# First norm's shift row summed on TensorE, four tiles scaled by ScalarE, and another order of the gate and up products

## The chip, the cores and the metric

The kernel runs on one core of one Trainium2 chip. The metric is the device time of one execution in microseconds (us). Before the change it is 2370.89 us, the median of three runs (2370.7 to 2372.88).

## The reference

The reference is a trunk of two layers on x of 1024 rows (tokens) by 1024 columns in float32, with a conditioning vector c of 1024. Cut to what matters here:

```python
c_act = silu(c)
for l in range(2):
    mod = (c_act @ ada_w[l] + ada_b[l])            # 6 * 1024 values
    sh1, sc1, g1, sh2, sc2, g2 = split(mod, 6)
    h = rms_norm(x, norm1_w[l]) * (1.0 + sc1) + sh1
    proj = h @ w_in[l]                             # 1824 columns
    ... three head groups: windowed attention, latent attention, spatial gating
    x = x + g1 * (y @ w_out[l])
    h = rms_norm(x, norm2_w[l]) * (1.0 + sc2) + sh2
    gate, up = split(h @ w_gate_up[l], 2)          # 2 * 2816 columns
    x = x + g2 * ((silu(gate) * up) @ w_down[l])
return rms_norm(x, final_norm_w)
```

The change touches two places: the first norm of layer 0, with `sc1` and `sh1` and the first projection's start, and the products of gate and up in both layers.

## The kernel before

**Arithmetic.** Large products are made of float32 values that are split in a high part, rounded to the fast float32 form, and a low part, the rest. `mm3` then issues three matmuls for one: high by high (L134), low by high (L135), high by low (L136). A part of 128x512 is one matmul. Operands that are split need two instructions: a cast to the high part (ACT, `TH`, `gus`) and a subtraction for the low part (`sub`, L139, `TL`).

**First norm of layer 0.** The 1024 rows are eight tiles of 128. Each tile is loaded (`load_x0`, L229), normalised on ACT (`normalise`, L235 and L237) and transposed on PE (`transposed`, L294, eight 128x128 pieces in two PSUM banks `hT`), and ACT copies the two banks to SBUF (`xT`, L295). The modulation comes from `ada_w`: for the shift (j = 0) and the scale (j = 1), and for each half of 512 columns, four loads of 256 rows by 512 columns, 512 KB each (`ada0w`, L265). Each brings two blocks of 128 rows, and DVE multiplies each with a value of `c_act` per partition and adds it up (`ada_mac`, L254 and L256, 32 in all). At the end of a half `reduce0` transposes the sums on PE (L281), DVE adds up over what were partitions (L283) and adds the bias (L284, and L286 for the scale). The result, `mod0`, holds a scale and a shift for each column of x, one value per partition after the transpose. `modulate` then scales a half of a tile: four pieces by DVE (L613), the high part by ACT (L616), the low part by POOL (L139).

**The first projection.** `w_in`'s columns 512 to 1023 come first (`wr`, loaded by `load_w1` at L570, split to `wh` and `wl`). Each tile needs 24 matmuls on its bank `avq`: twelve for the first half of the modulation, twelve for the second. `avq_end` evacuates a tile by three instructions of ACT (L649, L651, L655) and a DMA (`cq`, L652). Tiles 0 to 3 (`NE` = 4) can begin with the first half of the modulation alone; the others, and their loads of x, come behind both halves.

**Order.** Each engine works its instructions in the program's order. For the start of layer 0 that order is written out by hand in the string `PRS`: each letter stands for one step of a sequence (X a load of x, N a normalisation, t a tile's transposes, a and b the sums of the two halves, r a reduction, m a modulation, l a load of `w_in`, s a split, h, v, G, B the projections). `need("r", 2)` lets a sequence run another one up to a step. A buffer is held back until some work is done by a copy of one element (`after`, L304): DVE writes it to the buffer that a DMA will fill, so SP, which issues all DMAs here one after the other, waits for DVE at that point.

**Gate and up.** The gate and up product is a scheme with seven products in place of eight per pair of column blocks (11 pairs a layer). `left` yields the seven operands, of which some are sums and differences made on POOL; ACT casts and DVE subtracts to split them. A product is 24 matmuls, 12 to a bank `gate` and 12 to a bank `up`. Three pairs of banks are in use: `yy`, `xx` and `vv`. `yy` accumulates products 0, 3, 4 and 5, `vv` products 2 and 6, and `xx` product 1. Between two products of `yy` ACT copies its state out (`u`, L1523 after product 3, L1528 after product 4; `p1` after product 0).

Of the kernel before, what the change touches and what calls it, by code (L numbers as in the profile page):

```python
# [49 lines left out]
PRS = "XtaaaaNtNsatNlrbthmhmbhasmbNbGmbbNllblCmtmmsbmNhtGvaamrtvvmvmNmmGvvNmBBGsvBCBv"  # L50
SP0 = (1, 1, 0, 0)
MA = (0, 0, 0, 0)
# [14 lines left out]
EY = (1, 0, 1, 1, 0, 0, 0, 1)  # L67
AHEAD = (4, 2, 6, 10, 7, 9, 9)
# [10 lines left out]
def tile_trunk(ctx, tc, x, c, positions, ada_w, ada_b, norm1_w, w_in, a_sinks, b_q_norm_w, b_w_uq,  # L79
# [50 lines left out]
    def f32(t):  # L130
        return t.bitcast(F32)
# [117 lines left out]
    acc0 = {j: G([P, D], F32, "acc0") for j in (1, 0)}  # L249
# [20 lines left out]
    def macs0(raws, hf):  # L270
        for j, kp, raw in raws:
            a = acc0[j][:, hf * 512:(hf + 1) * 512]
            for k in range(2):
                ada_mac(a, raw[:, k, :], 2 * kp + k)
            yield

    def reduce0(hf):
        for j in (1, 0):
            pt = PA("ada0")
            for i in range(4):  # L280
                PE.transpose(chunk(pt, i), chunk(acc0[j], 4 * hf + i), ident)  # L281
            d = slice(8 * j + 4 * hf, 8 * j + 4 * hf + 4)
            DVE.reduce_sum(out=mod0[:, d], in_=pt.rearrange("p (a b) -> p a b", a=4), axis=AX.X)  # L283
# [5 lines left out]
    def transposed(xn):  # L289
        r = G([P, KD, P], F32, "xT")  # L290
        for kh in range(2):
# [3 lines left out]
            ACT.copy(out=r[:, 4 * kh:4 * kh + 4], in_=pv)  # L295
# [257 lines left out]
    def layer(l, x_tiles):  # L553
# [49 lines left out]
        def modulate(t, kh):  # L603
# [4 lines left out]
            for kk in range(4 * kh, 4 * kh + 4):  # L608
                if kk - 4 * kh < MA[2 * (t >= NE) + kh]:
                    ACT.activation(out=xa[:, kk, :], in_=xa[:, kk, :], func=AF.Identity, scale=mod0[:, 8 + kk:9 + kk],  # L610
                                   bias=mod0[:, kk:kk + 1])
                else:
# [4 lines left out]
            sub(POOL, lo[:, ks_], xa[:, ks_], f32(h[:, ks_]))  # L617
# [40 lines left out]
        if l == 0:  # L658
# [17 lines left out]
            def t_seq():  # L676
                for t in range(NT):
                    need("N", t + 1)
                    xT0[t] = transposed(xns.pop(t))
                    yield  # L680
# [725 lines left out]
        def left(a11, a12, a21, a22, tmp, tt):  # L1406

            yield a11
            yield a12
            tt(a11, a11, a21, ALU.subtract)  # L1410
            yield a11
            tt(tmp, a22, a11, ALU.subtract)
            yield tmp
            tt(a21, a21, a22, ALU.add)
            yield a21
            tt(a12, a12, tmp, ALU.subtract)
            yield a12
            yield a22
# [42 lines left out]
        def gu_prep(raws):  # L1461
            gens = []
            for r0, r1 in raws:
                tmp = AD("s2").rearrange("p (k c) -> p k c", k=4)
                gens.append(left(r0[:, :, 0, :], r1[:, :, 0, :], r0[:, :, 1, :], r1[:, :, 1, :], tmp, tt_on(POOL)))
# [16 lines left out]
        def gu_pair(j, ops, ahead):  # L1482

            p1 = G([P, 2, 512], F32, "p1")
            u4, u2 = [None, None], [None, None]
# [4 lines left out]
            def products(i, name, ps, first):  # L1490
                ahead(i)
                w = ops(i)
# [12 lines left out]

            yy = banks()
            yield from products(0, "b11", yy, True)
            for m in range(2):
                ACT.copy(out=p1[:, m, :], in_=yy[m])
            yield  # L1510
            xx = banks()
            yield from products(1, "b21", xx, True)
            for m in range(2):
                DVE.tensor_tensor(out=p1[:, m, :], in0=p1[:, m, :], in1=xx[m], op=ALU.add)
            finish(p1[:, 0, :], p1[:, 1, :], 0, 0)
            yield
            vv = banks()
            yield from products(2, "t3", vv, True)
            yield
            yield from products(3, "t2", yy, False)  # L1520
            for m in range(2):
                u2[m] = SM([P, 512], F32, "u2")
                ACT.copy(out=u2[m], in_=yy[m])  # L1523
            yield
# [258 lines left out]
```

## Time and profile before

| what | before |
|---|---|
| median of three runs | 2370.89 us |
| the profiled execution, its own time | 2370.5 us |
| its span | 2368.8 us |
| mean granted TensorE clock | 0.983 |
| first matmul of the first projection | at 33.19 us |
| second half of the modulation complete | at 51.4 us |
| last matmul of the first projection | from 95.32 us |
| gate and up, layer 0 and layer 1 (the windows read) | 531 to 987 and 1705 to 2143 us |

The profile is one execution, and its times are counted from the span's start. In a timeline a row gives the start, the time from there to the end, the engine, the line, the operation, what it writes and reads, how many instructions the row holds, and in brackets the idle time of the engine before it with what ended it. SPq rows are DMA issues. In a table of windows the columns are the window's ends, its length, the busy time and number of instructions of PE, PEld (weight loads), DVE, ACT and POOL, the granted TensorE clock as a share of the full one, the busy share of the DMA engines and GB/s. In a list of waits stand the us in total, the number of waits and the longest.

### The profile page before, as it was taken

How to read it: one execution, taken by the hardware profiler on the slowest of the kernel's cores; microseconds unless marked ns; L12 is line 12 of the kernel's file. 1: busy time of each engine (PE TensorE's matmuls, PEld its weight loads, DVE VectorE, ACT ScalarE, POOL GpSimd, SP SyncE). 2: the span in 40 equal slices, each digit the busy share in tenths (PEclk: the TensorE clock that was granted, in tenths of full speed). 3: DMA queues.
4: the chain of work that ended last, by engine and by line, in shares of the span. 5: the costliest groups of instructions: out<-in, count | busy, mean ns of one | idle time of the engine just before them, and what ended most of it. 6: DMA issues, size and time to landing. Idle time of an engine off the chain costs nothing. (4 is left out here: it accounts for less than half of the span.)

```text
span 2368.8 us, 31988 instructions
## 1 busy us (share of the span) xinstructions
PE 2258.4 (95%) x11191; PEld 1904.2 (80%) x11191; DVE 1775.4 (75%) x2793; ACT 1120.9 (47%) x2296; POOL 984.8 (42%) x997
## 2 busy tenths in 40 slices
PE   5999899999999999999999899999999999999998
PEld 4789798887888777878878788988878888887786
DVE  7787578848767777699974875687588767638978
ACT  4566377636344344323344654784564444432233
POOL 4766630322323324545554655212224334225643
PEclk9999999999999999999999999999999999999999
DMA  6503432212566565862240253222134544468433
GB/s 255 167 19 110 175 132 90 90 54 89 173 213 232 186 232 187 319 253 89 80 158 19 62 172 143 81 81 98 54 110 177 180 169 169 171 223 287 150 109 114
DMA packets 155397, 347.66 MB, mean 147 GB/s; under 512 B 12522, under 2 KB 71652, under 8 KB 155236
## 3 DMA queue, kind: packets, MB, share of 16 engines
q1 hardware_dynamic: 155236, 345.62, 42.2%
q8 instruction: 88, 1.44, 0.3%
q14 instruction: 73, 0.60, 0.1%
HBM read 250.65 MB, written 94.92 MB: 146 GB/s over the span
## 5 line engine op out<-in xcount | busy, mean ns | idle before, releaser
L139 DVE TENSOR_TENSOR gus<-gur,gus 128x512 fp32r<-128x512 f32 x264 | 248.3, 961 | 60.3 <-ACT gus L142 59.5
L142 ACT CAST gus<-gur 128x512 fp32r<-128x512 f32 x264 | 160.7, 624 | 209.7 <-PE gate L136 77.0
L134 PE MATMUL gate<-hTh,gus 128*128 128x512 f32 x616 | 243.9, 396 | 15.2 <-ACT hTh L142 8.1
L134 PE MATMUL down<-dnt,dns 128*128 128x512 f32 x616 | 241.8, 393 | 11.5 <-issue 6.0
L134 PE MATMUL up<-hTh,gus 128*128 128x512 f32 x616 | 241.1, 391 | 3.8 <-ACT u L1528 3.8
L135 PE MATMUL down<-dnt,dns 128*128 128x512 f32 x616 | 241.1, 391 | 1.3 <-DVE dnt L139 1.3
L135 PE MATMUL gate<-hTl,gus 128*128 128x512 f32 x616 | 241.7, 392 | 0.1
L136 PE MATMUL gate<-hTh,gus 128*128 128x512 f32 x616 | 241.2, 392 | 0.0
L136 PE MATMUL down<-dnt,dns 128*128 128x512 f32 x616 | 240.7, 391 | 0.0
L136 PE MATMUL up<-hTh,gus 128*128 128x512 f32 x616 | 240.4, 390 | 0.0
L135 PE MATMUL up<-hTl,gus 128*128 128x512 f32 x616 | 240.2, 390 | 0.0
L1435 POOL TENSOR_TENSOR gur<-gur 128x512 f32<-128x512 f32 x44 | 65.2, 1482 | 398.8 <-DVE gus L139 369.5
L142 ACT CAST dns<-act 128x512 fp32r<-128x512 f32 x132 | 81.8, 622 | 248.6 <-PE down L136 189.6
L1613 DVE TENSOR_TENSOR x<-x,down 128x512 f32<-128x512 f32 x224 | 148.0, 679 | 28.9 <-PE down L136 28.6
L134 PEld LDWEIGHTS gate<-hTh,gus 128*128 128x128 f32 x616 | 116.9, 190 | 43.4 <-ACT u L1523 10.0
L139 DVE TENSOR_TENSOR dns<-act,dns 128x512 fp32r<-128x512 f32 x132 | 136.3, 1047 | 15.5 <-ACT dns L142 15.3
L134 PEld LDWEIGHTS down<-dnt,dns 128*128 128x128 f32 x616 | 116.2, 189 | 38.5 <-issue 6.8
L134 PEld LDWEIGHTS up<-hTh,gus 128*128 128x128 f32 x616 | 116.1, 189 | 28.7 <-ACT u L1528 4.9
L135 PEld LDWEIGHTS down<-dnt,dns 128*128 128x128 f32 x616 | 116.5, 189 | 25.8 <-DVE dnt L139 1.7
L135 PEld LDWEIGHTS gate<-hTl,gus 128*128 128x128 f32 x616 | 116.8, 190 | 25.2 <-DVE hTl L139 1.5
L136 PEld LDWEIGHTS gate<-hTh,gus 128*128 128x128 f32 x616 | 116.7, 189 | 24.5
L136 PEld LDWEIGHTS down<-dnt,dns 128*128 128x128 f32 x616 | 116.5, 189 | 24.5
(415 smaller groups left out, 6132.8 us busy)
## 6 DMA issues: line engine op xcount, KB each, us to landing
gur<-in_w_gate_up_dram SPq DMA_DIRECT2D x88, 512.0 KB
ada<-in_ada_w_dram SPq DMA_DIRECT2D x80, 512.0 KB
wp<-wpe SPq DMA_DIRECT2D x77, 512.0 KB
dnt<-wp SPq DMA_DIRECT2D x77, 512.0 KB
dnr<-in_w_down_dram SPq DMA_DIRECT2D x44, 512.0 KB
act<-act SPq DMA_DIRECT2D x44, 512.0 KB
wr<-in_w_in_dram SPq DMA_DIRECT2D x24, 512.0 KB
act<-u SPq DMA_DIRECT2D x44, 256.0 KB
```

The costliest lines, as they stand in the source:

```text
L134: PE.matmul(ps, lh, rh, start=start, stop=False, skip_group_check=more)
L135: PE.matmul(ps, lh, rl, start=False, stop=False, skip_group_check=more)
L136: PE.matmul(ps, ll, rh, start=False, stop=stop, skip_group_check=more)
L139: eng.tensor_tensor(out=out_, in0=a, in1=b, op=ALU.subtract)
L142: ACT.copy(out=h, in_=src)
L1435: return lambda o, a, b, op: eng.tensor_tensor(out=o, in0=a, in1=b, op=op)
L1613: DVE.tensor_tensor(out=av_, in0=av_, in1=ps[t], op=ALU.add)
```

## The change

1. **Shift row.** `acc0` is there for the scale alone. For the shift, `macs0` issues eight matmuls per load (four chunks of 128 columns, two row blocks each): a 128x128 float32 chunk of the load is the stationary operand and the column of `cact` the moving one, and the result is one column of a PSUM tile `sh0`. There are 64 of them, and 16 products of DVE fall away. `reduce0` sums `sh0` directly, without transposes.
2. **Tiles 4 to 7.** Their transposed pieces are scaled by ACT as it reads them from PSUM, eight activations of 128x128 (L313) in place of two copies; DVE's 32 scalings of these tiles (L613 before, L629 after) fall away, and their transposes now wait for both halves of the modulation.
3. **Low parts** in `modulate`: 16 subtractions of 128x512 go from POOL to DVE.
4. `load_w1` waits for the sums of the scale (`acc0[1]`) in place of those of the shift, and in `PRS` some steps stand elsewhere.
5. **Gate and up.** From the second pair on the seven products run as 0, 2, 3, 1, 4, 6, 5, the first pair's as 0, 1, 2, 3, 4, 6, 5, and the last one, 5, runs behind product 0 of the next pair. ACT copies `vv` after product 2 (`v2`), and DVE adds `yy` to that copy after product 4; before, ACT copied `yy` after product 4 and DVE added `vv`. The number of instructions is the same.

The core of the diff:

```diff
-PRS = "XtaaaaNtNsatNlrbthmhmbhasmbNbGmbbNllblCmtmmsbmNhtGvaamrtvvmvmNmmGvvNmBBGsvBCBv"
+PRS = "XtaaaaNtNsatNlrbthmhmbhasmbNbGmbbNllblCmmmsbmNhGvaamrtvtvmvmNmmtGvvNmtBBGsvBCBv"
+ORD = ((0, 1, 2, 3, 4, 6, 5), (0, 2, 3, 1, 4, 6, 5))
...
-    acc0 = {j: G([P, D], F32, "acc0") for j in (1, 0)}
+    acc0 = {1: G([P, D], F32, "acc0")}
+    sh0 = PA("sh0")
...
     def macs0(raws, hf):
         for j, kp, raw in raws:
+            if j == 0:
+                for i in range(4):
+                    c = 4 * (4 * hf + i) + kp
+                    for k in range(2):
+                        PE.matmul(sh0[:, c:c + 1], chunk(raw[:, k, :], i), cact[:, 2 * kp + k:2 * kp + k + 1],
+                                  start=(k == 0), stop=(k == 1))
+                yield
+                continue
...
-    def transposed(xn):
+    def transposed(xn, modulated):
...
-            ACT.copy(out=r[:, 4 * kh:4 * kh + 4], in_=pv)
+            if not modulated:
+                ACT.copy(out=r[:, 4 * kh:4 * kh + 4], in_=pv)
+                continue
+            for k in range(4):
+                kk = 4 * kh + k
+                ACT.activation(out=r[:, kk, :], in_=pv[:, k, :], func=AF.Identity, scale=mod0[:, 8 + kk:9 + kk],
+                               bias=mod0[:, kk:kk + 1])
...
-            sub(POOL, lo[:, ks_], xa[:, ks_], f32(h[:, ks_]))
+            sub(DVE, lo[:, ks_], xa[:, ks_], f32(h[:, ks_]))
...
+                    if t >= NE:
+                        need("r", 2)
+                    xT0[t] = transposed(xns.pop(t), t >= NE)
...
-                    raw_w.append(load_w1(kp, acc0[0]))
+                    raw_w.append(load_w1(kp, acc0[1]))
...
+            for n, i in enumerate(ORD[j > 0]):
+                if i == 0:
+                    yy = banks()
+                elif i == 1:
+                    xx = banks()
+                elif i == 2:
+                    vv = banks()
+                yield from products(n, ("b11", "b21", "t3", "t2", "t1", "b22", "t4")[i],
+                                    xx if i == 1 else vv if i in (2, 6) else yy, i < 3)
...
+                elif i == 2:
+                    for m in range(2):
+                        v2[m] = SM([P, 512], F32, "v2")
+                        ACT.copy(out=v2[m], in_=vv[m])
...
+                elif i == 4:
+                    for m in range(2):
+                        DVE.tensor_tensor(out=v2[m], in0=v2[m], in1=yy[m], op=ALU.add)
+                    finish(v2[0], v2[1], 1, 1)
...
         for j in range(1, NJ):
-            drain(pair_steps(j))
+            g = pair_steps(j)
+            run(g, 2)
+            drain(open_pair.pop())
+            drain(first_products(g, 5))
+        drain(open_pair.pop())
```

How the instructions stand, at three places. First, PE at the start of the program, up to the first matmul of the first projection (`avq`), before:

```order
L294 MATMUL hT_420<-ident,xn_413 128x128 x4
L294 MATMUL hT_426<-ident,xn_413 128x128 x4
L294 MATMUL hT_450<-ident,xn_434 128x128 x4
L294 MATMUL hT_456<-ident,xn_434 128x128 x4
L281 MATMUL ada_50_479<-ident,acc_9_158 128x128 x4
L281 MATMUL ada_51_487<-ident,acc_10_159 128x128 x4
L294 MATMUL hT_513<-ident,xn_464 128x128 x4
L294 MATMUL hT_519<-ident,xn_464 128x128 x4
L134 MATMUL avq_537<-wh_443,TH_529 128x512
```

and of the change, where three more rows like the first (loads 366, 370 and 374) stand ahead of these:

```order
L277 MATMUL sh_10_159<-cact,ada0w_378 128x1 x8
L307 MATMUL hT_432<-ident,xn_425 128x128 x4
L307 MATMUL hT_438<-ident,xn_425 128x128 x4
L307 MATMUL hT_462<-ident,xn_446 128x128 x4
L307 MATMUL hT_468<-ident,xn_446 128x128 x4
L292 MATMUL ada_50_503<-ident,acc_9_158 128x128 x4
L307 MATMUL hT_532<-ident,xn_476 128x128 x4
L307 MATMUL hT_538<-ident,xn_476 128x128 x4
L277 MATMUL sh_10_159<-cact,ada0w_515 128x1 x8
L277 MATMUL sh_10_159<-cact,ada0w_519 128x1 x8
L277 MATMUL sh_10_159<-cact,ada0w_523 128x1 x8
L134 MATMUL avq_556<-wh_455,TH_548 128x512
```

The matmuls of the first half's four shift loads now stand ahead of the transposes of tiles 1, 2 and 3 (the three pairs of `hT` rows), and those of three of the second half's four loads ahead of the projection.

Second, the SP queue behind the first half's ada loads, before (`wr` are loads of `w_in`, `ada0w` those of `ada_w`):

```order
L229 DMA x_380<-in_x_dram 128x1024
L570 DMA wr_440<-in_w_in_dram 128x2x512
L570 DMA wr_470<-in_w_in_dram 128x2x512
L265 DMA ada0w_494<-in_ada_w_dram 128x2x512
L265 DMA ada0w_496<-in_ada_w_dram 128x2x512
```

and of the change:

```order
L229 DMA x_380<-in_x_dram 128x1024
L589 DMA wr_452<-in_w_in_dram 128x2x512
L589 DMA wr_482<-in_w_in_dram 128x2x512
L589 DMA wr_619<-in_w_in_dram 128x2x512
L266 DMA ada0w_513<-in_ada_w_dram 128x2x512
```

The third load of `w_in`, which stood behind the second half's eight ada loads, now stands ahead of them. What releases the three is on DVE, here in the change (before, the first two copies stood behind nine products, of both sums, and had no reduction ahead of them):

```order
L255 TENSOR_SCALAR acc_9_158<-ada0w_364,cact 128x512
L257 SCALAR_TENSOR_TENSOR acc_9_158<-ada0w_364,cact,acc_9_158 128x512
L257 SCALAR_TENSOR_TENSOR acc_9_158<-ada0w_368,cact,acc_9_158 128x512
L296 TENSOR_REDUCE mod_160<-sh_10_159 128x4
L257 SCALAR_TENSOR_TENSOR acc_9_158<-ada0w_368,cact,acc_9_158 128x512
L297 TENSOR_TENSOR mod_160<-mod_160,vcol 128x4
L323 COPY wr_452<-acc_9_158 1x1
L257 SCALAR_TENSOR_TENSOR acc_9_158<-ada0w_372,cact,acc_9_158 128x512 x2
L323 COPY wr_482<-acc_9_158 1x1
L257 SCALAR_TENSOR_TENSOR acc_9_158<-ada0w_376,cact,acc_9_158 128x512 x2
L323 COPY wr_619<-acc_9_158 1x1
```

The copies that release the three loads stand behind the reduction of the first half's shift sums (L296).

Third, PE around the transposes of tile 7 (`hT`, the last two such rows of either program; the first projection's matmuls of tile 5 are `avq_974` before, those of tile 4 `avq_990` after). Before:

```order
L134 MATMUL avq_974<-wh_734,TH_873 128x512
L135 MATMUL avq_974<-wl_735,TH_873 128x512
L136 MATMUL avq_974<-wh_734,TL_874 128x512
L294 MATMUL hT_1010<-ident,xn_913 128x128 x4
L294 MATMUL hT_1016<-ident,xn_913 128x128 x4
```

and of the change, where `avq_796` is tile 3:

```order
L136 MATMUL avq_796<-wh_759,TL_627 128x512
L307 MATMUL hT_881<-ident,xn_790 128x128 x4
L307 MATMUL hT_890<-ident,xn_790 128x128 x4
L307 MATMUL hT_966<-ident,xn_953 128x128 x4
L307 MATMUL hT_975<-ident,xn_953 128x128 x4
L134 MATMUL avq_990<-wh_455,TH_782 128x512
```

Tile 7's transposes stood behind the products of tiles 4 and 5; now they stand, with tile 6's, ahead of them.

More of the change, by code (lines that the diff above doesn't have):

```diff
@@ L278, in reduce0 @@
         for j in (1, 0):
-            pt = PA("ada0")
-            for i in range(4):
-                PE.transpose(chunk(pt, i), chunk(acc0[j], 4 * hf + i), ident)
             d = slice(8 * j + 4 * hf, 8 * j + 4 * hf + 4)
-            DVE.reduce_sum(out=mod0[:, d], in_=pt.rearrange("p (a b) -> p a b", a=4), axis=AX.X)
+            if j == 1:
+                pt = PA("ada0")
+                for i in range(4):
+                    PE.transpose(chunk(pt, i), chunk(acc0[j], 4 * hf + i), ident)
+                sums = pt.rearrange("p (a b) -> p a b", a=4)
+            else:
+                sums = sh0[:, 16 * hf:16 * hf + 16].rearrange("p (a b) -> p a b", a=4)
+            DVE.reduce_sum(out=mod0[:, d], in_=sums, axis=AX.X)
             DVE.tensor_tensor(out=mod0[:, d], in0=mod0[:, d], in1=vcol[:, d], op=ALU.add)
@@ L607, in modulate @@
             xa = xT0[t]
[L608 to L612, printed above, removed]
+            if t < NE:
+                for kk in range(4 * kh, 4 * kh + 4):
                     DVE.tensor_scalar(out=xa[:, kk, :], in0=xa[:, kk, :], scalar1=mod0[:, 8 + kk:9 + kk],
@@ L1402, in norm2_b, with left @@
                         ACT.activation(out=d, in_=pv[:, i, :], func=AF.Identity, scale=a, bias=b)
[L1406 to L1418, printed above, removed]
+        def left(a11, a12, a21, a22, tmp, tt, order=range(7)):
+            for i in order:
+                if i == 2:
+                    tt(a11, a11, a21, ALU.subtract)
+                elif i == 3:
+                    tt(tmp, a22, a11, ALU.subtract)
+                elif i == 4:
+                    tt(a21, a21, a22, ALU.add)
+                elif i == 5:
+                    tt(a12, a12, tmp, ALU.subtract)
+                yield (a11, a12, a11, tmp, a21, a12, a22)[i]
         def right(b11, b12, b21, b22, tmp, tt):
@@ L1459, in load_gu, with gu_prep @@
             return r
-        def gu_prep(raws):
+        def gu_prep(raws, order):
             gens = []
@@ L1464, in gu_prep @@
                 tmp = AD("s2").rearrange("p (k c) -> p k c", k=4)
-                gens.append(left(r0[:, :, 0, :], r1[:, :, 0, :], r0[:, :, 1, :], r1[:, :, 1, :], tmp, tt_on(POOL)))
+                gens.append(left(r0[:, :, 0, :], r1[:, :, 0, :], r0[:, :, 1, :], r1[:, :, 1, :], tmp, tt_on(POOL), order))
             for srcs in zip(*gens):
@@ L1504, in finish @@
                 DMA.dma_start(out=actd[l][2 * j + m][:, b, :], in_=g)
[L1506 to L1524, printed above, removed]
-            yield from products(4, "t1", yy, False)
-            for m in range(2):
-                u4[m] = SM([P, 512], F32, "u4")
-                ACT.copy(out=u4[m], in_=yy[m])
-            for m in range(2):
-                DVE.tensor_tensor(out=u4[m], in0=u4[m], in1=vv[m], op=ALU.add)
```

58 lines of the change are left out of this document (37 added, 21 removed).

## The prediction

> **What bounds the kernel now.** The page comes first, then a table of stretches of the span, then the sequence of rows at the start and the list of waits. On the page:
>
> ```profile
> span 2368.8 us, 31988 instructions
> PE 2258.4 (95%) x11191; PEld 1904.2 (80%) x11191; DVE 1775.4 (75%) x2793; ACT 1120.9 (47%) x2296; POOL 984.8 (42%) x997
> PE   5999899999999999999999899999999999999998
> ```
>
> PE is busy 95% of the span; only the first of forty slices (59 us each) is at 5 tenths. The time is PE's work plus what PE waits for, and a change pays by filling PE's gaps or costs by opening new ones. By stage (columns: length, then busy us of PE, PEld, DVE, ACT and POOL, then granted clock, DMA share, GB/s):
>
> ```profile
> 0.00:33.18 33.18, 10.35 (x42) 8.20 (x42) 18.38 (x35) 17.40 (x25) 12.59 (x69) 1.00 0.94 355
> 33.18:44.95 11.77, 11.62 (x36) 8.56 (x36) 11.77 (x20) 3.07 (x5) 8.48 (x4) 1.00 0.46 164
> 44.95:51.42 6.47, 3.08 (x18) 2.80 (x19) 6.43 (x12) 3.72 (x6) 2.90 (x5) 0.88 0.00 0
> 51.42:95.69 44.27, 41.48 (x183) 33.46 (x183) 31.14 (x78) 28.05 (x62) 26.73 (x30) 0.94 0.57 180
> 95.69:122.40 26.71, 23.32 (x106) 18.77 (x104) 25.90 (x30) 7.03 (x15) 20.93 (x17) 0.94 0.36 123
> 531.00:987.00 456.00, 440.33 (x1948) 360.63 (x1947) 345.55 (x416) 196.86 (x353) 153.28 (x101) 0.99 0.58 197
> 1705.00:2143.00 438.00, 431.94 (x1906) 356.42 (x1905) 307.74 (x373) 202.04 (x357) 156.48 (x103) 0.99 0.48 168
> ```
>
> The first five rows are the first norm and its projection, the last two the gate and up stages of the layers. Until 33.18 the DMAs are the limit (share 0.94), and PE idles 23 us. At 44.95 PE stops again: DVE is busy 6.43 of 6.47 us with the last sums of the modulation. From 51.42 PE is full.
>
> **The first load chain.** The start of the kernel in order of time; an SPq row is a DMA issue.
>
> ```profile
> 2.25 1.31 SPq L229 DMA_DIRECT2D x<-in_x_dram  x3
> 5.78 1.06 ACT L235 ACTIVATE xn<-x 128x1024 f32<-128x1024 f32 x1 [2.97 <-DMA x<-in_x_dram]
> 9.08 1.97 PE L294 MATMUL hT<-ident,xn 128*128 128x128 f32 x8 [5.31 <-ACT xn L237]
> 11.44 0.49 DVE L254 TENSOR_SCALAR acc<-ada0w,cact 128x512 f32<-128x512 f32 x1 [0.69 <-DMA ada0w<-in_ada_w_dram]
> 14.90 1.97 PE L294 MATMUL hT<-ident,xn 128*128 128x128 f32 x8 [3.85 <-ACT xn L237]
> 17.23 0.19 DVE L304 COPY wr<-acc 1x1 f32<-1x1 f32 x2
> 17.35 4.06 DVE L256 SCALAR_TENSOR_TENSOR acc<-ada0w,cact,acc 128x512 f32<-128x512 f32 x6
> 17.39 0.88 SPq L570 DMA_DIRECT2D wr<-in_w_in_dram  x2
> 18.32 5.82 SPq L265 DMA_DIRECT2D ada0w<-in_ada_w_dram  x8
> 21.07 1.97 PE L294 MATMUL hT<-ident,xn 128*128 128x128 f32 x8 [4.19 <-ACT xn L237]
> 33.19 0.80 PE L134 MATMUL avq<-wh,TH 128*128 128x512 f32 x1 [4.02 <-ACT TH L616]
> ```
>
> The first shift load is there at 11.44. The small copies of L304 at 17.23 let SP issue the first w_in loads, and right behind them the second half of the ada loads, at 18.32. The eight first-half loads land one after the other, the last at about 19.5: 11.44 and six more at 1.3 us, 512 KB at the 0.94-busy queues.
>
> The new one-column matmuls are not in this program's start, but their like is elsewhere:
>
> ```profile
> 1359.38 0.73 PE L548 MATMUL sq<-ones,yA 128*128 128x1 f32 x6
> 1361.32 1.28 PE L548 MATMUL sq<-ones,yA 128*128 128x1 f32 x6
> 1360.62:1364.03 3.41, 3.41 (x16) 3.41 (x15) 1.86 (x7) 2.81 (x9) 2.63 (x3) 0.50 0.92 286
> 1364.03:1367.45 3.42, 3.42 (x16) 3.42 (x15) 3.36 (x7) 0.48 (x1) 1.28 (x3) 0.50 0.74 240
> ```
>
> Three f32 matmuls of the program are six records, two passes each: 0.73 / 6.5 = 0.112 us a pass at full clock, 1.28 / 6 = 0.213 at half. A load's 8 matmuls are 16 passes: 1.8 us or 3.4 us. Which of them? The transposes at 9.08 took 1.97 for 8 passes (0.25), those further on 1.03 (row 83.23 below), so the start runs at half. And the window from 1360.62, in which PE was busy throughout, with one-column matmuls among the others, still left the next one at 0.50. I take 3.4, with 1.8 as the other end.
>
> By the Trainium skill, "TensorE: Matmul & The Clock Gate", section "What's actually happening", about 3.4 us of sustained activity releases the half rate. By that rule the clock would be full after the first load's matmuls; the row from 1360.62 does not agree, being full in time and followed by a half window.
>
> **Part one, the shift sums on PE.** PE takes the four shift loads in a row behind tile 0's transposes and ahead of tile 1's: 11.4 + 4 x 3.4 = 25.0 (or 19.5 + 1.8 = 21.3 at full clock, where the last landing decides). DVE takes the reduction of these sums after its third product, ahead of the small copies. A reduction, a product (4.06 / 6 = 0.68) and two short instructions, 1.7 us: first copy at 26.7, the next two at 28.2 and 29.7 (two products apart each). SP's three w_in loads wait for these and stand ahead of the eight ada loads, which therefore go out from 29.8 (26.0) instead of 18.32. From issue to first use are 3.5 us (x: 2.25 to 5.78), then 1.3 us a load, so the second-half shift loads are there at 35, 37.5, 40 and 43 (31 to 39). The queues, 0.94 busy before, lie idle some 6 us.
>
> Tile 1's transposes start at 25.0 instead of 14.90; the next tiles follow 6.2 us apart (14.90 to 21.07), so tile 3's end at 25.0 + 12.4 + 2.0 = 39.4 (34.7). Three second-half shift loads stand behind them on PE and ahead of the first projection matmul: 39.4 + 3 x 3.4 = 49.6 (40.1). First projection matmul: **49.6** instead of 33.19. Its 36 matmuls took 11.8 us (second row of the table), to 61.4 (8.2 us if the clock is warm, to 48.3). Then the last shift load 1.8, and what follows the last transposes of the sums:
>
> ```profile
> 48.97 0.63 PE L281 MATMUL ada<-ident,acc 128*128 128x128 f32 x4 [0.82 <-DVE acc L256]
> 51.27 0.15 DVE L286 SCALAR_TENSOR_TENSOR mod<-mod,vcol 128x4 f32<-128x4 f32 x1
> ```
>
> 48.97 to 51.42 is 2.4 us, so the second half of the modulation is complete at 61.4 + 1.8 + 2.4 = **65.6** instead of 51.4 (full clock 52.5). DVE is relieved of 16 products x 0.68 = 10.9 us; that is costed at nothing here, because the loads and PE now end later than DVE.
>
> **Part two, tile 7.** Rows from there on, and two groups of the stretch from 33 to 96:
>
> ```profile
> 52.91 9.31 DVE L613 TENSOR_SCALAR xT<-xT,mod 128x128 f32<-128x128 f32 x19
> 59.85 0.35 SPq L229 DMA_DIRECT2D x<-in_x_dram  x1
> 75.14 0.66 SPq L229 DMA_DIRECT2D x<-in_x_dram  x1
> 83.23 1.03 PE L294 MATMUL hT<-ident,xn 128*128 128x128 f32 x8
> 507.44 2.90 ACT L1402 ACTIVATE hb<-hT,modc 128x128 f32<-128x128 f32 x8
> L651 ACT COPY cq<-avq 128x384 f32<-128x384 f32 x7 | 3.6, 509 | 0.0
> L655 ACT ACTIVATE junk<-avq 128x384 f32<-128x384 f32 x7 | 3.7, 527 | 0.0
> ```
>
> Before, tile 7's transposes come 83.23 - 51.4 = 31.8 us after the modulation, and PE spends that on tiles 0 to 5. In the changed order tile 6's and tile 7's transposes stand ahead of tile 4's products, so PE has only 60 matmuls (the second halves of tiles 0 to 2, all of tile 3) and 24 transposes: 60 x 0.226 (440.33 / 1948 in the table) and 24 x 0.13 (1.03 / 8), 17 us. The chain to tile 7 is no shorter: 8.5 to tile 6's x (51.4 to 59.85), 3.5 landing, 3.3 from there to the transposes (5.78 to 9.08), 1.5 for these and the first scaling's wait; now 16 scalings on ACT ahead of the evacuation that SP waits for, 16 x 0.35 = 5.5 (2.90 for eight); 3 for the evacuation of tiles before it (0.51 and 0.53 an instruction, with two shorter ones) and 1 on SP; again 3.5 and 3.3: 33 us. PE idles 33 - 17 = **16 us**, and loses 1.7 more in a half-clock window after it. Bounds: 0 if the x load does not wait behind the scalings, 20 if it does and the small DMAs slip too. DVE takes the low parts, 16 of 128x512 at some 0.68 = 11 us, and loses the scaling of four tiles, 32 at up to 0.49 (9.31 / 19) = 16: no cost. Behind tile 7 stand 96 matmuls.
>
> So the last projection matmul ends at 65.6 + 33 + 1 + 1.7 + 21.8 (96 x 0.226) = 123, against 95.7 (last row 95.32 + 0.39):
>
> ```profile
> 95.32 0.39 PE L136 MATMUL avq<-wh,TL 128*128 128x512 f32 x1
> ```
>
> That is 27 later; full clock 52.5 + 57.5 = 110, 14 later. Some is won back up to 122.4, where DVE is busy 25.9 of 26.7 us with work that is partly independent of the projection and PE idles 3.4: I take 7 of 27 back (5 of 14). **Stage one +20**, ends 0 (no stall) and +25.
>
> **Part three, gate and up.** What PE waits for in layer 0's stage, and in layer 1's:
>
> ```profile
> PE gate L134 <- ACT u L1523: 6.3, 5, 1.8
> PE up L134 <- ACT u L1528: 3.8, 2, 2.1
> PE gate L134 <- ACT hTh L142: 4.1, 1, 4.1
> PE gate L134 <- ACT u L1523: 0.6, 1, 0.6
> 776.94:780.35 3.41, 3.41 (x9) 2.64 (x9) 2.96 (x4) 0.02 (x1) 0.61 (x1) 0.50 0.26 85
> ```
>
> L1523 and L1528 are the copies that free a pair of PSUM banks which the very next product writes. In the new order another product stands between for pairs 1 to 10 (24 matmuls, 12 to a bank, 24 x 0.226 = 5.4 us), and the longest wait was 2.1. At most 6.3 + 3.8 + 0.6 goes, and the half-clock window at 776.94 behind such a wait (1.7 us): -12.4. In pair 0 the order stays, and DVE (345.55 of 456) still makes the operands at the same pace, so part of the copies' lateness can return as a wait for operands: I take **-8**; the other end is +5, one new wait as long as a product.
>
> **Sum.** 2370.5 (profiled execution: span 2368.8 and 1.7 around it; median of the runs 2370.9) + 20 - 8 = 2382.5, said as **2383 us**.
>
> **Rivals.** *A, DVE was the limit.* At 44.95 PE waited for DVE, and DVE loses 11 us of products ahead of the modulation. If the shift matmuls run at 0.112 behind the loads, the w_in copies come when they came (the reduction waits for the last landing alone, 19.5), and tile 7's load slips past the scalings, stage one costs 3 at most and may win 3, and all 12 of part three are won: 2370.5 - 12 and 3 to either side, 2355 to 2361. It decides from the point where stage one costs under 8, since then part three outweighs it. Against it stand the orders of SP and PE. 0.18. *B, the shift matmuls warm the clock, the stall stays.* PE is busy from 11.4 without a break; if a busy window counts whatever is in it, the passes go at 0.112 after the first load: the full-clock ends above, 14 later less 5 won back, +9, and -8: 2372, no change. The row from 1360.62 speaks against it. 0.12. (It is the rule of the Trainium skill that is named above.) *C, the change does not do in gate and up what its order says.* DVE paces the operands, and the waits removed at the copies come back as waits for operands: 0 to +5 there, +25 in stage one: 2396 to 2401. For it speaks DVE's 76% in that stage; against it, that PE's list there has no wait for an operand but the first. 0.12.
>
> **Chances.** Forecast 0.58, A 0.18, B 0.12, C 0.12. The forecast's own range is 2374 to 2392, by the two ends of the stall and the clock; into the cases of A and C the range goes from 2357 to 2398. A measurement of this kernel tells about 0.2% (4.7 us) from no change. Of the forecast's 0.58, 0.04 may fall short of that, half of it beyond: slower 0.54 + 0.12 = 0.66, same 0.12 + 0.02 = 0.14, faster 0.18 + 0.02 = 0.20.
>
> **What would show it.** Right: the first avq matmul near 50 instead of 33.19; eight ada loads issued near 30 instead of 18.32; the modulation's second half near 65; PE idle some 16 us in one piece ahead of tile 7's transposes; the last avq matmul near 120; no wait on u in gate and up above 1 us. Wrong: first avq matmul by 40 with shift matmuls stepping at 0.112; no gap ahead of tile 7; or waits for gus in gate and up in place of those for u.

## The result, and the profile after

The changed kernel takes 2386.93 us, the median of four runs (2384.28 to 2387.9), against 2371.89 for the kernel before on the same chip. The ratio is 1.0059 with a 95% interval of 1.0045 to 1.0073: slower by 0.6%. The forecast was 2383 us, with a range of 2357 to 2398. The page's head after the change:

```profile
span 2386.1 us, 32148 instructions
PE 2276.7 (95%) x11311; PEld 1927.8 (81%) x11311; DVE 1756.6 (74%) x2761; ACT 1122.8 (47%) x2320; POOL 946.4 (40%) x981
PE   7799989998999999999999998999999999999998
```

PE's first slice has risen from 5 to 7, and this is no gain: the new matmuls fill it. DVE and POOL have become lighter, by 19 and 38 us, and the time has gone up. The start of the kernel in order of time:

```profile
9.13 1.97 PE L307 MATMUL hT<-ident,xn 128*128 128x128 f32 x8 [5.26 <-ACT xn L237]
11.57 13.81 PE L277 MATMUL sh<-cact,ada0w 128*128 128x1 f32 x64 [0.48 <-DMA ada0w<-in_ada_w_dram]
25.42 0.17 DVE L296 TENSOR_REDUCE mod<-sh 128x4 f32<-128x16 f32 x1 [11.41 <-PE sh L277]
26.46 3.87 SPq L589 DMA_DIRECT2D wr<-in_w_in_dram  x3
30.38 6.20 SPq L266 DMA_DIRECT2D ada0w<-in_ada_w_dram  x8
39.43 10.40 PE L277 MATMUL sh<-cact,ada0w 128*128 128x1 f32 x48 [0.28 <-DMA ada0w<-in_ada_w_dram]
49.69 0.77 PE L134 MATMUL avq<-wh,TH 128*128 128x512 f32 x1
60.85 1.84 PE L277 MATMUL sh<-cact,ada0w 128*128 128x1 f32 x16
64.19 0.15 DVE L299 SCALAR_TENSOR_TENSOR mod<-mod,vcol 128x4 f32<-128x4 f32 x1
87.39 0.37 SPq L229 DMA_DIRECT2D x<-in_x_dram  x1
94.63 1.97 PE L307 MATMUL hT<-ident,xn 128*128 128x128 f32 x8 [14.19 <-ACT xn L237]
121.88 0.39 PE L136 MATMUL avq<-wh,TL 128*128 128x512 f32 x1
```

Four shift loads are 64 passes in 13.81 us, 0.216 a pass: half rate, for the whole 13.8 us in which PE did nothing else and never paused. The last shift load, behind 36 matmuls of 512 columns (the row at 60.85), ran its 16 passes in 1.84 us, 0.115 a pass: full rate. DVE waited 11.41 us for these sums. The second-half loads of `ada_w` left at 30.38 instead of 18.32, the first projection matmul came at 49.69 instead of 33.19, and the modulation was complete at 64.3 instead of 51.4. Then 14.19 us of idle PE stand ahead of tile 7's transposes. The projection ended at 122.3 instead of 95.7.

By stage (length, busy us of PE, PEld, DVE, ACT and POOL, granted clock, DMA share, GB/s):

```profile
11.57:25.38 13.81, 13.80 (x65) 13.81 (x66) 0.83 (x2) 1.97 (x4) 0.74 (x2) 1.00 0.63 243
80.44:94.63 14.19, 0.00 (x0) 0.00 (x1) 2.08 (x3) 11.86 (x34) 3.18 (x9) 0.60 0.52 178
94.63:122.30 27.67, 26.15 (x108) 21.59 (x109) 17.52 (x26) 11.12 (x27) 3.01 (x6) 0.90 0.38 134
122.30:143.30 21.00, 21.00 (x105) 17.60 (x103) 9.81 (x22) 5.98 (x14) 13.16 (x14) 1.00 0.19 60
552.00:1011.00 459.00, 441.10 (x1947) 362.69 (x1946) 352.35 (x417) 192.00 (x354) 155.44 (x101) 0.99 0.56 196
2166.00:2378.00 212.00, 209.83 (x923) 172.51 (x921) 183.00 (x228) 68.47 (x118) 104.24 (x71) 1.00 0.45 161
```

The first row shows a limit of the clock column: it reads 1.00 there, as it did over the start of the kernel before, though the matmuls step at 0.216 us a pass where the same ones took 0.115 later. In such a place the rate is to be read from the matmuls. In the second row PE is empty and ACT busy 11.86 of 14.19 us; the gap is the time in which ACT scales tiles 5 and 6, evacuates, and tile 7's x comes.

How far the changed program runs behind the one before, at the same matmul in both traces (differences of starts and ends that each trace gives):

| place | us behind |
|---|---|
| first matmul of the first projection | +16.5 |
| its last matmul | +26.6 |
| first score matmul (122.4 before) | +20.9 |
| first gate matmul, layer 0 | +20.8 |
| first down matmul, layer 0 | +23.8 |
| last matmul of layer 1's first projection | +20.8 |
| first gate matmul, layer 1 | +24.7 |
| first down matmul, layer 1 | +23.0 |
| last down matmul | +17.4 |

The first norm costs 20.8 us net. Gate and up in layer 0 did not gain: +3, which came back up to the end of layer 1's first projection, most of it in layer 0's down stage. Another 5.6 us came back in the last down stage of layer 1, where nothing was expected. What PE, ACT and DVE waited for in layer 0's gate and up after the change (us in total, times, longest):

```profile
PE gate L134 <- ACT u L1547: 7.8, 2, 4.1
PE up L134 <- ACT u L1547: 4.0, 2, 2.2
ACT gus L142 <- DVE acc L257: 55.6, 20, 7.5
DVE acc L257 <- DMA ada<-in_ada_w_dram: 25.9, 17, 4.8
```

Before, the waits on copies were 10.1 us in seven, none above 2.1. Now there are 11.8 us in four, up to 4.1 each, although a whole product stands between the copy and the next use of its bank. The copy (`u`, L1547, behind product 3) comes still later than that: it stands in ACT's order behind casts that wait. Ahead of the longest wait:

```profile
951.82 1.14 ACT L142 CAST gus<-gur 128x512 fp32r<-128x512 f32 x2 [7.46 <-DVE acc L257]
952.86 0.58 ACT L1547 COPY u<-gate 128x512 f32<-128x512 f32 x1
```

Ahead of each of the other three copies, too, a cast had waited, 3.3 to 5.2 us.

### The profile page after: what moved, and what is told of

It is laid out like the page before. It is cut to its first block, busy times and chain, and to the rows that moved or that the text cites. A ratio compares the mean times of both kernels' runs of the same rounds, so it can differ in the third digit from the quotient of the medians.

```text
span 2386.1 us, 32148 instructions
## 1 busy us (share of the span) xinstructions
PE 2276.7 (95%) x11311; PEld 1927.8 (81%) x11311; DVE 1756.6 (74%) x2761; ACT 1122.8 (47%) x2320; POOL 946.4 (40%) x981
## 5 line engine op out<-in xcount | busy, mean ns | idle before, releaser
L139 DVE TENSOR_TENSOR gus<-gur,gus 128x512 fp32r<-128x512 f32 x264 | 235.6, 907 | 117.6 <-ACT gus L142 113.0
L134 PEld LDWEIGHTS down<-dnt,dns 128*128 128x128 f32 x616 | 115.6, 188 | 35.5 <-ACT dns L142 6.1
L1452 POOL TENSOR_TENSOR gur<-gur,s 128x512 f32<-128x512 f32 x44 | 68.0, 1552 | 183.0 <-DVE gus L139 183.0
L135 PEld LDWEIGHTS up<-hTl,gus 128*128 128x128 f32 x616 | 116.1, 188 | 24.0
```

What stands on the lines that cost most here:

```text
L134: PE.matmul(ps, lh, rh, start=start, stop=False, skip_group_check=more)
L135: PE.matmul(ps, lh, rl, start=False, stop=False, skip_group_check=more)
L139: eng.tensor_tensor(out=out_, in0=a, in1=b, op=ALU.subtract)
L1452: return lambda o, a, b, op: eng.tensor_tensor(out=o, in0=a, in1=b, op=op)
```

## The experiments

Each ratio is taken against the kernel before on the same chip, whose median was 2370.90 to 2374.66 us in these runs. So the ratios and the traces are to be compared, and the medians only with that in mind.

### The two parts apart

The first run has the changed first norm with the gate and up code of before; the second has it the other way round.

The edits to the changed kernel, of the first run and of the second (each undoes the whole part of which it shows the head):

```diff
-ORD = ((0, 1, 2, 3, 4, 6, 5), (0, 2, 3, 1, 4, 6, 5))
...
```

```diff
-PRS = "XtaaaaNtNsatNlrbthmhmbhasmbNbGmbbNllblCmmmsbmNhGvaamrtvtvmvmNmmtGvvNmtBBGsvBCBv"
+PRS = "XtaaaaNtNsatNlrbthmhmbhasmbNbGmbbNllblCmtmmsbmNhtGvaamrtvvmvmNmmGvvNmBBGsvBCBv"
...
```

> The changed first norm with the gate and up order of before. Theory (the first norm costs 20.8 us by the time the gate and up stage of layer 0 starts, and nothing of it comes back): 2370.5 + 21 = 2391 to 2393, the last matmul of the first projection at 122, waits on u in layer 0's gate and up as before (10 us). Rival (the two parts of the change hang together, and the late start is given back in gate and up): 2387 or less.

> The first norm of before with the changed gate and up order. Theory (in the changed kernel the distance of its stages from those of before goes from +20.8 ahead of the first gate and up to +17.3 at the end, of which layer 0's gate and up takes +3 and layer 1's -1.7): 2370.5 - 3.5 = 2367, with some 10 us of waits on u left in layer 0. Rival one (the waits in layer 0 come from the late start alone): 2362, no wait on u above 1 us. Rival two (the order costs): 2373.

The first norm alone: 2392.93 us, ratio 1.0075 (1.006 to 1.009), which is 14 to 21 us. Its trace runs 21.0 us behind at the first gate matmul, 20.2 at layer 1's first projection and 18.7 at the end: the first norm's cost stays, and PE's waits on `u` in layer 0 are 9.8 us (10.1 before). Gate and up alone: 2365.18 us, ratio 0.9961 (0.9947 to 0.9976), which is a gain of 0.4%, 6 to 13 us. Its trace is 2.7 us behind at layer 0's first down matmul, level at layer 1's first projection (0.0), and 6.2 ahead at the end. PE's waits in layer 0's gate and up of the second run:

```profile
PE gate L135 <- ACT u L1530: 10.3, 2, 6.0
PE up L135 <- ACT u L1530: 1.6, 1, 1.6
```

So those 11.9 us are there without the late start, and rival one falls on that. By where the time goes in the traces the theory holds in both runs; by the times it does not quite. The first run's interval reaches from the rival's bound (16 us) to the theory's 21, and the second run gained more than the theory's 3.5, as much as rival one had. The changed program's distance is not quite the sum of the two: 18.7 - 6.2 = 12.5 against 17.4 in the traces, 0.75 - 0.39 = 0.36% against 0.59% in the times, where each of the three has an interval of some 0.15% to either side. In the traces most of what is left over arises between layer 1's first projection and its gate and up, where the changed program lost 3.9 us (20.8 to 24.7) and run one 0.2. Run two and four of the runs below, which have the changed gate and up (shift row on DVE, sums at other positions, tile 7 late, wide matmuls), lost 0.5 to 0.8 in that stretch of the program. In the changed program's trace a half-clock stretch of 6.8 us stands there, in code that is not touched:

```profile
1332.44:1339.27 6.83, 6.78 (x25) 5.99 (x26) 3.43 (x7) 2.15 (x5) 4.22 (x6) 0.50 0.00 0
```

Half of 6.83 is 3.4 us, so that stretch accounts for most of it; why it fell there in this trace was not tried.

### The shift row on DVE again

The sums of the shift are made by DVE as before; everything else is the changed kernel.

```diff
-    acc0 = {1: G([P, D], F32, "acc0")}
-    sh0 = PA("sh0")
+    acc0 = {j: G([P, D], F32, "acc0") for j in (1, 0)}
...
     def macs0(raws, hf):
         for j, kp, raw in raws:
-            if j == 0:
-                ...
```

> The changed kernel, but the shift row is summed by DVE as before; tiles 4 to 7 are still scaled by ACT, low parts on DVE, the same order string. Theory (the one-column matmuls cost 14 us at the modulation and the order around tile 7 another 13): the first projection matmul at about 35, the modulation's second half at about 54, a gap of 10 to 14 us ahead of tile 7's transposes, and 2387 - 12 = 2375. Rival (the matmuls alone do it, and tile 7 waits only because they hold back the loads): no gap, 2387 - 21 = 2366.

2373.0 us, ratio 0.9997 (0.9986 to 1.0008): against the changed kernel's 1.0059, 0.62% or 14.7 us are gone, which is nearer the theory's 12 than the rival's 21. In the trace, three places:

```profile
31.34 0.80 PE L134 MATMUL avq<-wh,TH 128*128 128x512 f32 x1 [1.19 <-ACT TH L619]
39.58 0.79 PE L136 MATMUL avq<-wh,TL 128*128 128x512 f32 x1 [7.01 <-DVE TL L139]
83.44 1.97 PE L294 MATMUL hT<-ident,xn 128*128 128x128 f32 x8 [15.01 <-ACT xn L237]
```

The projection starts at 31.34, even ahead of before, and the modulation is complete at 52.5. The gap ahead of tile 7 is there in full, 15.0 us, without any one-column matmul: it is a cost of its own. The second row is a cost that the prediction put at zero: with both sums and the low parts on DVE, the third matmul of the projection waits 7.0 us for a low part. In the changed kernel PE has no such wait: there the late start covers it.

### Tile 7's transposes behind the products of tiles 4 and 5

One letter of the changed kernel's order string is moved.

```diff
-...mNmmtGvvNmtBBGsvBCBv"
+...mNmmGvvtNmtBBGsvBCBv"
```

> The changed kernel with one letter of the order string moved: tile 7's transposes stand behind the products of tiles 4 and 5 again. Theory (the gap of 14.2 us comes from that place in PE's order, not from ACT's scaling): 48 matmuls or 10.9 us of products go in front, the gap shrinks to some 3 us, the projection ends near 110 instead of 122.3; as part of that was given back before, 2387 - 8 = 2379. Rival (the scaling on ACT holds the x load and PE back wherever tile 7 stands): a gap of over 10 us, 2385 or more.

2377.78 us, ratio 1.0028 (1.0016 to 1.0041), 0.31% or 7.4 us under the changed kernel; the theory said 8. What PE waits for there, first this kernel:

```profile
PE avq L134 <- ACT TH L632: 2.0, 1, 2.0
PE hT L307 <- ACT xn L237: 0.8, 1, 0.8
```

and the changed kernel between 80 and 123 us:

```profile
PE hT L307 <- ACT xn L237: 14.2, 1, 14.2
```

The gap of 14.2 us is gone (2.0 and 0.8 are left), and the projection ends at 108.0 instead of 122.3. ACT still scales tiles 4 to 7. The place in the order made the gap, and the scaling did not.

### All of the first norm's suspects undone but the scaling

Shift row on DVE, low parts on POOL, tile 7 late; ACT still scales tiles 4 to 7 out of PSUM, and gate and up are in the changed order.

```diff
-    acc0 = {1: G([P, D], F32, "acc0")}
-    sh0 = PA("sh0")
+    acc0 = {j: G([P, D], F32, "acc0") for j in (1, 0)}
...
-            sub(DVE, lo[:, ks_], xa[:, ks_], f32(h[:, ks_]))
+            sub(POOL, lo[:, ks_], xa[:, ks_], f32(h[:, ks_]))
...
-...mNmmtGvvNmtBBGsvBCBv"
+...mNmmGvvtNmtBBGsvBCBv"
```

> The changed gate and up order and the scaling of tiles 4 to 7 on ACT, but the shift row on DVE, the low parts on POOL, and tile 7's transposes behind the products of tiles 4 and 5. Theory (the cost of the changed first norm is all in the one-column matmuls, DVE's low parts behind its sums, and tile 7's place): as with the first norm of before, 2365, within 3. Rival (the scaling on ACT out of PSUM, and transposes that wait for both halves, cost by themselves): 2370 or more.

2367.24 us, ratio 0.9981 (0.9971 to 0.999), against 0.9961 with the first norm of before. In the trace the projection ends 3.1 us behind the kernel before and the first gate matmul comes 2.6 behind. In the trace the theory holds within its 3 us; by the ratios the two runs are 0.2% (4.7 us) apart, with intervals that overlap. A rest of some 2.6 us stays with the scaling on ACT and the order string, too little to take apart in these runs.

### The clock: wide matmuls for the same sums

The column of c becomes the stationary operand and 512 columns of the load the moving one; a half's sums stand in one row, which eight small matmul records turn into columns at its end.

```diff
-                for i in range(4):
-                    c = 4 * (4 * hf + i) + kp
-                    for k in range(2):
-                        PE.matmul(sh0[:, c:c + 1], chunk(raw[:, k, :], i), cact[:, 2 * kp + k:2 * kp + k + 1],
-                                  start=(k == 0), stop=(k == 1))
+                for k in range(2):
+                    PE.matmul(shr[hf][0:1, :], cact[:, 2 * kp + k:2 * kp + k + 1], raw[:, k, :],
+                              start=(kp == 0 and k == 0), stop=(kp == 3 and k == 1))
```

> The changed kernel, but the shift row is summed with the column of c as the stationary and 512 columns of the load as the moving operand, two matmuls a load into one row, which is turned into columns at the half's end. Theory (the clock follows the columns moved, not the busy time): the granted clock is full from the second window behind 11.5, a load takes 1.7 us or less, the first projection matmul comes near 40 instead of 49.7, and the time falls by 6 to 10, to 2379. Rival (a wide float32 matmul is as dear as eight narrow ones, or the clock stays at half): first projection matmul at 47 or later, time within 3 of 2387.

2379.6 us, ratio 1.0038 (1.0023 to 1.0053), 0.21% or 5 us under the changed kernel; the intervals of the two overlap (1.0045 to 1.0073 there), so the gain is not certain by the times. The rows:

```profile
12.38 6.28 PE L275 MATMUL shr<-ada0w,cact 128*1 128x512 f32 x8 [1.36 <-DMA ada0w<-in_ada_w_dram]
19.61 3.60 PE L275 MATMUL shr<-ada0w,cact 128*1 128x512 f32 x8
33.17 0.80 PE L134 MATMUL avq<-wh,TH 128*128 128x512 f32 x1 [1.19 <-ACT TH L635]
87.42 1.97 PE L310 MATMUL hT<-ident,xn 128*128 128x128 f32 x8 [13.65 <-ACT xn L237]
```

Eight records, two loads, took 6.28 us at first and the next eight 3.60. Record by record, the first six start 0.85 us apart without a pause, those from 19.61 on 0.43 apart; the change of rate comes at about 17.8, 5.4 us behind the first wide matmul. The one-column matmuls of the changed kernel kept PE as busy for 13.8 us and stayed at 0.216 a pass. So a full PE does not release the half rate here; wide matmuls do. What in them counts (the columns moved, or fewer weight loads between them) was not taken apart. By the Trainium skill, "TensorE: Matmul & The Clock Gate", section "What's actually happening", a busy window of about 3.4 us is enough. This run agrees with it for wide matmuls; the changed kernel's 13.81 us do not for one-column ones, and the measurement decides. The run does not give the clock's share of the saving by itself, since the wide form also has fewer instructions and stands otherwise in PE's order: the projection began at 33.17, better than the 40 expected. It gave less back than that start promised: the gap ahead of tile 7 (13.65 us) remains, and a wait of 4.5 us for DVE's low parts has come up.

### Why the copies in gate and up are still late

Four runs look for it, the first with the changed first norm and the other three with that of before. First, the sums for the next modulation (`ada_bg`: DVE multiplies and adds loads of `ada_w`, L257) are taken at positions 1, 3, 4 and 6 of a pair, as in the kernel before; the change had moved them to positions 0 to 3, which the list of the change above does not name.

```diff
-                    if 7 * (j - 1) + i < 9 or i < 4:
+                    if 7 * (j - 1) + i < 9 or i in (1, 3, 4, 6):
                         run(bg)
```

> The changed kernel, but in gate and up the sums for the next modulation are run at positions 1, 3, 4 and 6 of a pair's products, as before, and not at 0 to 3. Theory (these sums, taken in a row, hold ACT's casts and so the copies of u back for over 5.4 us): the waits on u in layer 0 (11.8 us) fall under 4, and the time by 8 to 12, to 2375 to 2379. Rival (it is the order of ACT's casts and copies, whatever the sums do): waits and time as they are, 2387 within 2.

2389.2 us, ratio 1.0062 (1.0046 to 1.0079), the same as the changed kernel's. PE's waits on the copies in layer 0 moved to other pairs but stayed at 10.1 us in sum (11.8 in the changed kernel). The theory fell: that the sums are taken in a row is not the cause.

Second, the loads of those sums get buffers of another ring than the operands.

```diff
-            raw = W([P, D], F32, "ada")
+            raw = G([P, D], F32, "ada")
```

> The first norm of before and the changed gate and up order; the loads for the next modulation's sums go to buffers of another ring than the operands of gate and up. Theory (ACT's cast to a buffer that such a load had last waits for DVE's sum, and this for its DMA; ACT's copies of u stand behind that cast): the waits of ACT's casts on DVE's sums (55 us) fall under 15, the waits on u in layer 0 (11.9 us) under 4, and the time by 8 to 10 to 2356. Rival (DVE, in order, is late with these sums whichever buffer they have): waits move to the operands, time within 2 of 2365.

2365.7 us, ratio 0.9978 (0.9969 to 0.9987), as with the changed gate and up alone. ACT's list, after this edit:

```profile
ACT gus L143 <- DVE acc L257: 7.3, 1, 7.3
ACT wpe L143 <- DVE acc L257: 28.3, 5, 8.1
```

and PE's:

```profile
PE gate L135 <- ACT u L1530: 11.6, 5, 3.4
```

The `gus` casts' waits on DVE's sums fell from 55 to 7.3 us, as expected, and PE's waits on the copies stayed at 11.6. But ACT's other waits rose: those of the `wpe` casts on the sums from 10.6 to 28.3, and those of the `gus` casts on a DMA that the profile names `wp` from 10.1 to 33.3. So the theory fell as far as the ring goes: giving the loads another one moves ACT's waits and does not bring the copies earlier.

Third, most of the sums are taken out of the stage and run behind it.

```diff
-                    if 7 * (j - 1) + i < 9 or i < 4:
+                    if 7 * (j - 1) + i < 13:
                         run(bg)
```

> The first norm of before and the changed gate and up order; of the sums for the next modulation only the first 13 steps stand in layer 0's gate and up, the rest behind its last pair. Theory (DVE, in order, waits for the loads of these sums and so is late with ACT's and POOL's inputs; the copies of u are late for that): no wait on u in layer 0 above 1 us, as in layer 1, and layer 0's gate and up takes 447 to 450 us from its first matmul to its last instead of 458; what the sums cost behind it is not part of the bet. Rival (ACT is late by its own order of casts): waits on u of 8 us or more and 456 us or more.

The stage of layer 0 now takes 437 us from its first matmul to its last, and PE is busy for nearly all of it; ahead of this, with the changed gate and up alone, 458.5. The theory said 8 to 11 us less, and it is 21. First this run, then that one:

```profile
534.00:971.00 437.00, 431.47 (x1909) 356.24 (x1908) 324.98 (x382) 190.95 (x342) 142.28 (x93) 0.99 0.50 175
```

```profile
531.00:989.50 458.50, 441.14 (x1949) 362.93 (x1947) 351.23 (x418) 192.29 (x353) 155.49 (x102) 0.98 0.56 196
```

PE's idle time in the stage fell from 17.4 to 5.5 us (length less PE's busy time), of which 4.1 is the wait at its start, and no wait on a copy is left. PE's busy time fell by 9.7 us as well: the sums' own transposes are out of the stage, and so are two half-clock stretches of 6.8 us that lay at the waits. The kernel as a whole takes 2388.53 us (1.0070, 1.0055 to 1.0085), since the sums now stand in a block behind the stage. So the theory holds for the stage as far as this: with all of these sums in it the copies are late, and with their first 13 steps alone they are not. The edit takes out DVE's work, its loads and their buffers together, and does not tell which of them does it. Layer 1, which has no such sums, has no wait on a copy in the changed order either.

Fourth, with the order 0, 1, 2, 3, 4, 6, 5 (below), these loads are issued two ahead.

```diff
-            if i + 1 < len(steps):
-                raw = load(*steps[i + 1])
+            if i + 2 < len(steps):
+                raws.append(load(*steps[i + 2]))
```

> As the run with the order 0, 1, 2, 3, 4, 6, 5 in all pairs and the first norm of before, and the loads for the next modulation's sums are issued two ahead instead of one. Theory (DVE waits for these loads, 13.7 us in that run, and passes it on to the copies of u): the wait of DVE's sums for loads falls under 4 us, the waits on u in layer 0 (8.3 us) under 4, and the time by 4 to 6, to 2357 to 2359, ratio 0.995 or less. Rival (one buffer more of the operands' ring goes to these loads, and the operands come later instead): 2363 or more.

2367.77 us, ratio 0.9983 (0.9971 to 0.9995). The sums' wait for their loads fell from 13.7 to 7.1 us, and the waits on the copies rose from 8.3 to 14.6:

```profile
DVE acc L257 <- DMA ada<-in_ada_w_dram: 7.1, 8, 2.3
PE gate L135 <- ACT u L1530: 13.9, 4, 4.3
PE up L135 <- ACT u L1530: 0.7, 1, 0.7
```

The time came out as the rival had it; whether for the rival's reason, the buffer that the loads take from the operands, these rows do not tell. Shorter waits for the loads alone do not bring the copies earlier. What is settled is that the copies are late when all the sums stand in the stage; which of DVE's time, the buffers and the queue of loads does it stays open.

### What the new order gains

First, all pairs in the order 0, 1, 2, 3, 4, 6, 5, with the last product still behind the next pair's first; the copies then have no product between again.

```diff
-ORD = ((0, 1, 2, 3, 4, 6, 5), (0, 2, 3, 1, 4, 6, 5))
+ORD = ((0, 1, 2, 3, 4, 6, 5), (0, 1, 2, 3, 4, 6, 5))
```

> The first norm of before; in gate and up all pairs run in the order 0, 1, 2, 3, 4, 6, 5, with the last one behind the next pair's first. Theory (the gain of the changed order is made in the down stage of layer 1, 5.6 us, by product 5 in the last place, and not by the place of product 1): 2365, as with the whole order. Rival (the order 0, 2, 3, 1 is what gains, the copies behind it being covered): 2371, as before.

2363.13 us, ratio 0.9969 (0.9957 to 0.998), as good as the whole order (0.9961). Moving product 1 gains nothing that can be measured. What is left does it: the place of products 5 and 6, and with it the copy of `vv` in place of `yy` and the other positions of the sums, which were not taken apart. In layer 0 its waits on the copies are 8.3 us:

```profile
PE gate L135 <- ACT u L1530: 7.3, 5, 2.0
PE up L135 <- ACT u L1530: 1.0, 1, 1.0
```

and its trace is 1.8 us ahead of before at the first down matmul, where the whole order was 2.7 behind.

Second, layer 0 as before and only layer 1 in the new order.

```diff
+        def order_of(j):
+            return range(7) if l == 0 else ORD[j > 0]
...
-        return gu_pair(j, lambda i: ready[7 * j + i], ahead)
+        return (gu_pair_old if l == 0 else gu_pair)(j, lambda i: ready[7 * j + i], ahead)
```

> The first norm of before; layer 0's gate and up as before, layer 1's in the changed order. Theory (layer 0's order gains nothing, since what it loses in its stage, 2.7 us, is given back by the start of layer 1): 2365, within 2. Rival (layer 0's loss is a loss): 2362 or less.

2366.37 us, ratio 0.9975 (0.9965 to 0.9984): within the theory's 2, and with an interval that overlaps that of the new order in both layers (0.9961). So no worth of the new order in layer 0 can be measured, and the gain is layer 1's: its trace is 0.8 us ahead at layer 1's first down matmul and 6.5 at the end. It is thus made in the down stage behind the last gate and up: from its first matmul to its last this takes 217.9 us before and 216.9 with the changed first norm alone, and 212.2 to 212.5 in every trace with the new order in layer 1. What that stage waited for before (its last 218 us):

```profile
PE down L134 <- ACT dnt L142: 3.0, 2, 1.5
PE down L134 <- issue: 2.5, 1, 2.5
```

and in the changed kernel:

```profile
PE down L134 <- ACT dnt L142: 1.6, 1, 1.6
PE down L134 <- ACT dns L142: 0.2, 1, 0.2
```

The waits fell from 5.5 to 1.8 us, and a half-clock window of 3.4 us at 2162.75 is gone, which costs half of it: 3.7 + 1.7 = 5.4, against 5.6 measured. The waits go with layer 1's order in the other traces too: with the order of before (the first norm alone) they are 6.0 us, with the new one (gate and up alone, and this run) 1.7. Which instruction of the new tail removes the wait of 2.5 was not tried.

## Why the prediction was right, and where not

**The first norm** went as its terms had it. First projection matmul 49.69 (forecast 49.6); ada loads issued at 30.38 (29.8); modulation complete at 64.3 (65.6); last projection matmul 122.3 (123); 26.6 us behind, of which 5.7 were won back (7 taken); net 20.8 (20). Inside this, misses cancel: the modulation was complete 1.3 us earlier than forecast, the chain to tile 7 took 2.7 us less, and what stands behind the gap 3.2 more (27.7 where the sum had 1 + 1.7 + 21.8), since half clock went on for 5.6 us there and PE waited another 1.5. The price of half rate for one-column matmuls, the choice on which the sum hung, was 0.216 a pass against 0.213 taken. The rival with a warm clock (B) fell on that row; in the run with wide matmuls the clock does come up in that place.

**The gap ahead of tile 7** was 14.2 us (16 forecast), and its cause the one named: the place of the transposes in PE's order. The run with one letter moved removes it. The chain to tile 7 took 30.3 us behind the modulation (33 in the sum): from tile 6's transposes to tile 7's load, 79.34 to 87.39, 8.1 us were needed where the sum had 11. The scaling on ACT is a link of that chain, as the sum said, but with tile 7 late it costs PE 2.0 us at most.

**DVE's low parts** were costed at zero. That is right in the changed kernel, where PE waits for none of them. Without the late start they cost a wait of 4.5 us (wide matmuls) or 7.0 (shift row on DVE, which has both sums to make then). The sentence named no cover that could go, and should have: the one-column matmuls were the cover.

**Gate and up** is the term whose mechanism failed, and its size is luck. The step is "At most 6.3 + 3.8 + 0.6 goes", worked out from the longest wait before (2.1) against a product of 5.4: in layer 0 none of the 10.1 us of waits went, 11.8 stood there after. A wait shows how long PE stood, not how late the copy is: the copies stood behind casts that had waited 3.3 to 7.5 us, so 5.4 us more of distance turned seven short waits into four long ones. The rival C had this mechanism in kind, in other words (waits for operands; they were waits for the copies), and its 0 to +5 in layer 0 is what came. The gain that did come, in layer 1's down stage, was in no term. As for the size, -8 was taken. From the stage's start to the end of the kernel the traces give -3.4 (+20.8 to +17.4), with some 3 us lost to the half-clock stretch at 1332.44; the run with gate and up alone gives -6.2 by its trace and -6 to -13 by its ratio.

So the forecast, 2383, is 4 us under the median. Trace against trace the program is 17.4 us behind where the sum had 12: 0.8 of that from the first norm, 4.6 from behind it, of which some 3 are that stretch. That the sum came so near rests in part on a gain made in another place than the one it was worked out for.

**Rival A** (DVE was the limit, and lightening it pays) fell: DVE lost 19 us in all, and the kernel got slower, since the sums of the shift and the loads behind them now ended later than DVE ever had.

## What to carry to other kernels

Work taken from a busy engine is paid for where it lands: see what stands behind it in the new engine's order, and which loads are released only at its end. Price matmuls with a few moving columns at the rate that PE has just before them: here they did not raise it by themselves. A wait in a list gives the time an engine stood, not the lateness of what it waited for: before costing a removed wait at its full length, follow the late instruction back on its own engine and see how far behind it runs.

## What the runs showed of the hardware that was not expected

13.8 us of one-column matmuls without a pause did not lift PE from half rate (64 passes at 0.216 us; 0.115 later, behind wide ones), while matmuls of 512 columns did within 5.4 us (from 0.85 to 0.43 us a record). And one trace lost some 3 us to a half-clock stretch in code that no edit touched, as at 1332.44, where five others lost 0.5 to 0.8: differences of that size in a single trace are no evidence of an edit.
